# Half of layer 0's output projection by Strassen's products, and three low parts of weight sums split by DMA

## The chip, the cores and the metric

The kernel runs on one core of one Trainium2 chip. The metric is the time of one execution on the device in microseconds (us), the median of several. Engines are named as in the profile: PE is TensorE's matmul, PEld its weight load, DVE is VectorE, ACT is ScalarE, POOL is GpSimd, SP is SyncE, which issues most DMAs.

## The reference

A trunk of two layers over 512 positions (S) with 1024 channels (D), all in float32. In layer 0 a projection gives four quarters of 512 channels; three make a gated convolution y_a, the fourth a multi-scale pooling y_b. Then comes the output projection, and after it the gated FFN with 2816 hidden channels.

```python
def gated_conv_ffn(x, w_gate, w_up, conv_w, conv_b, w_down):
    g = jnp.einsum('bsd,df->bsf', x, w_gate)
    g = causal_dwconv3(g, conv_w) + conv_b
    up = jnp.einsum('bsd,df->bsf', x, w_up)
    return jnp.einsum('bsf,fd->bsd', jax.nn.silu(g) * up, w_down)
...
        xn = rms_norm(h, norm_mix[layer])
...
            mix = jnp.concatenate([y_a, y_b], axis=-1)
            h = h + jnp.einsum('bse,ed->bsd', mix, w_out_even[i])
...
        hn = rms_norm(h, norm_ffn[layer])
        h = h + gated_conv_ffn(hn, w_ffn_gate[layer], w_ffn_up[layer], conv_ffn[layer],
                               b_conv_ffn[layer], w_ffn_down[layer])
```

Layer 1 has another mixer (gated spatial mixing in chunks) with its own output projection, and the same FFN. A last norm ends it.

## The kernel before, in words

**Numbers in two parts.** Every fp32 operand x of a matmul is held as hi, x rounded to the matmul's format, and lo, the rest x - hi. A product is three matmuls: hi·hi, hi·lo, lo·hi (mm3, lines 156 to 159). A split is usually an ACT copy for hi and a DVE subtraction for lo (parts, lines 149 to 154; halves, 791 to 793). The other way, by DMA: ACT writes the negated rounded copy into lo, a DMA issued by POOL adds x onto it (accumulate), ACT writes hi (summed, lines 138 to 146; lines 823 to 825). It takes the subtraction from DVE and gives one copy to ACT and one transfer to the DMA engines.

**The residual stream** h is eight tiles of 128 channels by 512 positions. Weights are fetched on SP's queue, in program order, into four raw buffers of 512 KB ("raw", line 131); a fetch waits until what was read from its buffer before has been used. Parts of weights have six buffers each (whi, wlo).

**Layer 0's mixer** ends with the products pm (y_b, the loop of mm_bank "pm"), the projection group "ab" (b_done: y_a), then project("oe", ...) (project, lines 303 to 317). It runs in two halves of four output tiles; a half is 8 contraction steps by 4 tiles by 3 = 96 matmuls of 512 columns, and its weights are four fetches of 512 KB. When a tile is finished, DVE adds it to h (line 315) and the norm splits the scaled h into hg (hi on ACT, line 202; lo on DVE, 203), squares it on ACT and sums the squares on POOL (213). The FFN's first step follows it on PE without a gap: "gu", FFN tiles 0 and 1 direct, whose fourth contraction step needs the norm's sums. Meanwhile the block sums and the weights of the next group are prepared.

**Seven products.** project_blocks (line 553) does one half of an output projection by Strassen's scheme, with 2 blocks of 256 positions, 2 of 512 input channels and 2 of 256 output channels: seven products instead of eight. Each is for two column blocks 4 steps x 3 = 12 matmuls of 256 columns (multiply, lines 622 to 645, the matmul at 642), 168 in all. It forms four sums of weights on DVE (to), splits seven weights, and adds each finished product onto h in halves of 256 (line 602). The moving operands are halves of the activations and four block sums (block_sums_of, lines 545 to 551, on DVE, in place). Before the change only the second half of layer 1's output projection goes this way ("oo1").

**The FFN** (class Ffn) goes through hidden tiles two at a time, f = 2, 4, ..., 20, each group again by Strassen's products for gate (g) and up (u): prepare(f) fetches four raw tiles (g and u, two halves of the input channels), forms in DVE the weight sums s12 and s34 for g and u, and splits them; products(f) runs the fourteen products in the order g1 u1 g2 g5 g6 u5 u6 g7 u2 u7 g3 u3 g4 u4, and after each an add onto rows or kept (line 865) or a copy (877). s34 holds the weights of products 7 and 3, the last sums to be formed; for up they are formed in the tile of s12 (line 834 and 836). For key "g" and f from 4 on, s12 and s34 are split by DMA; for "u" by ACT and DVE (the choice is by_dma). Where in_both holds (g from 4, u from 6; in group 4 also products 2, 5, 3 of u), a product is 4 matmuls of 512 columns, hi against both parts (line 632), and 4 of 256 with lo (635); else 12 of 256. Between the groups, the down projection takes the finished hidden tiles (d0_..., L157 to L159), with weight parts whi_d and wlo_d (lines 152, 153).

**Order.** Tile's scheduler decides how the instructions of each engine are ordered, from the program text and its own estimates; each engine then runs them strictly in that order, waiting on semaphores. So a change at one place can move instructions elsewhere. Tiles share pools: "four" has 5 buffers of 128 x 2 x 512, "sum" has 3, PSUM has 7 banks.

Of the kernel before, what the change touches and what calls it, by code (L numbers as in the profile page):

```python
# [8 lines left out]
F32 = mybir.dt.float32  # L9
F32R = mybir.dt.float32r  # L10
BF16 = mybir.dt.bfloat16
AF = mybir.ActivationFunctionType
ALU = mybir.AluOpType
PSUM = bass.MemoryType.PSUM

P = 128
D = 1024
S = 512
# [13 lines left out]
def tile_trunk(ctx: ExitStack, tc: tile.TileContext, x, norm_mix, norm_ffn, final_norm,  # L32
# [3 lines left out]
    nc = tc.nc  # L36
    x = x[0]
# [150 lines left out]
    hg = [(t[:, 0], t[:, 1]) for t in hg2]  # L188
# [74 lines left out]
    def split(pool, src, name, scale=1.0, tag="a", bufs=None):  # L263
        hi = pool.tile([P, S], F32R, tag=f"{tag}hi", bufs=bufs, name=f"{name}_hi")
        lo = pool.tile([P, S], F32R, tag=f"{tag}lo", bufs=bufs, name=f"{name}_lo")
        nc.scalar.activation(hi, src, AF.Copy, scale=scale)  # L266
        if isinstance(scale, float):
            nc.vector.tensor_tensor(lo, src, hi.bitcast(F32), ALU.subtract)
        else:
            nc.vector.scalar_tensor_tensor(lo, src, scale, hi.bitcast(F32),  # L270
                                           op0=ALU.mult, op1=ALU.subtract)
        return hi, lo
# [19 lines left out]
    def half_weights(name, w, ks, gi):  # L292

        chunks = {}
        for i in range(0, len(ks), 2):
            k0 = min(ks[i], ks[i + 1])
            hi, lo = weights(
                w[k0 * P : (k0 + 2) * P, gi * 512 : gi * 512 + 512]
                .rearrange("(k p) c -> p k c", p=P), 2, 512, f"{name}_{gi}_{k0}")
            chunks[k0], chunks[k0 + 1] = (hi, lo, 0), (hi, lo, 1)  # L300
        return chunks

    def project(name, w, acts, ks, norm, before=None, halves=(0, 1), tail=4):

        for gi in halves:
            chunks = half_weights(name, w, ks, gi)

            def lhs(k, j):
                hi, lo, n = chunks[k]
                cs = slice(j * P, (j + 1) * P)  # L310
                return hi[:, n, cs], lo[:, n, cs]

            def done(j, ps):
                k = gi * 4 + j
                nc.vector.tensor_tensor(h[k], ps, h[k], ALU.add)  # L315
                if norm is not None:
                    norm.add(k)

            group(f"{name}{gi}", range(4), ks, lhs, lambda k, j: acts[k], tail, done,
                  before if gi == 0 else None)  # L320


    prm0 = prm1 = None
# [10 lines left out]
    def in_group(name, w, c0, lhs_is_weight, on_done, tail, chunks=None, before=None,  # L334
                 after=(None, None), begun=None, after_later=None):
        if chunks is None:
            chunks = {}
            for k in range(0, NK, 2):
                in_parts(chunks, k, in_fetch(name, w, c0, k, 2),
                         after_later if k and after_later else after)  # L340

        def wt(k, j):
            cs = slice(j * P, (j + 1) * P)
            return chunks[k][0][:, cs], chunks[k][1][:, cs]

        def wt_wide(k, j):
            return chunks[k]

        def tokens(k, j):
            cs = slice(j * P, (j + 1) * P)  # L350
            return hg[k][0][:, cs], hg[k][1][:, cs]

        if lhs_is_weight:
            group(name, range(4), list(range(NK)), wt, lambda k, j: hg_k(k), tail, on_done, before,
                  begun=begun)
        else:
            group(name, range(4), list(range(NK)), tokens, wt_wide, tail, on_done, before)

    def mixer0():
        nonlocal prm0  # L360
        w = w_in_even[0]
        with tc.tile_pool(name="m0", bufs=1) as mp:
# [86 lines left out]
            mix = {}  # L449
# [3 lines left out]
            zs = {}  # L453
# [36 lines left out]
            prm0 = params0()  # L490
# [21 lines left out]
            cv = {}  # L512

            def v_done(j, ps):
                p = padded_tile()
                nc.vector.tensor_tensor(p[:, 2:], ps, ac[j], ALU.mult)
                if j % 2 == 0:
                    cv["pair"] = mp.tile([P, 2, S], F32, tag="four", bufs=5, name=f"cv{j}")
                t = cv["pair"][:, j % 2, :]
                conv3(t, p, *(prm0("ca", 4 * i + j) for i in range(3)))  # L520
                nc.gpsimd.tensor_tensor(t, t, rstd[0], ALU.mult)
                cv[j] = t

            in_group("av", w, 1024, True, v_done, 4)

            for g in range(4):
                ps = mm_bank(f"pm{g}")
                mm3(ps, (wpl_hi[:, g, :], wpl_lo[:, g, :]), pooled[g], True, True)
                mix[4 + g] = split(mp, ps, f"yb{g}", scale=prm0("psc", g), tag="mix", bufs=8)

            def b_done(j, ps):
                nc.vector.tensor_tensor(cv[j], ps, cv[j], ALU.mult)
# [2 lines left out]
            in_group("ab", w, 0, True, b_done, 4)  # L535

            nxt = Norm("f0", lambda k: prm0("ffn", k))
            project("oe", w_out_even[0], mix, [4, 5, 6, 7, 0, 1, 2, 3], nxt)
            return nxt


# [3 lines left out]
    def block_sums_of(y0, y1):  # L545

        t3, t1, t2, t4 = y1[:, :, HALF:], y0[:, :, HALF:], y0[:, :, :HALF], y1[:, :, :HALF]
        nc.vector.tensor_tensor(t3, t3, t1, ALU.subtract)
        nc.vector.tensor_tensor(t1, t1, t2, ALU.subtract)
        nc.vector.tensor_tensor(t2, t2, t3, ALU.add)  # L550
        nc.vector.tensor_tensor(t4, t4, t2, ALU.subtract)
# [57 lines left out]
    HALF = S // 2  # L609
    NP = NK // 2  # L610
    PAIRS = [k for i in range(NP) for k in (i, i + NP)]

    FIRST_WIDE = {"g": 4, "u": 6}

    BANK = {1: "a", 6: "a", 7: "a", 4: "a", 5: "e", 3: "e", 2: "b"}

# [36 lines left out]
    class Ffn:  # L653
# [141 lines left out]
        def prepare(self, f):  # L795

            layer, ap, n = self.layer, self.ap, f"{self.layer}_{f}"
            raws = ffn_weights(layer, f, [(key, half) for half in range(2) for key in "gu"])
            stat = {}

            def put(key, product, hi_lo, i):
                stat[key, product] = hi_lo[0][:, i], hi_lo[1][:, i]

            w = self.unit(f"a11_{n}")
            for i, key in enumerate("gu"):
                self.halves(w[0][:, i], w[1][:, i], raws[key, 0][0][:, :, :P])
                put(key, 1, w, i)
            for key in "gu":
                r0, r1 = raws[key, 0][0], raws[key, 1][0]
                s12 = ap.tile([P, 2, 4, P], F32, tag="sum", bufs=3, name=f"s12{key}_{n}")  # L810
                s34 = s12 if key == "u" else ap.tile([P, 2, 4, P], F32, tag="sum", bufs=3,
                                                     name=f"s34{key}_{n}")
                behind(nc.vector.tensor_tensor(s12[:, 0], r0[:, :, P:], r1[:, :, P:], ALU.add),
                       self.added[key])
                nc.vector.tensor_tensor(s12[:, 1], s12[:, 0], r0[:, :, :P], ALU.subtract)
                w = self.unit(f"s12{key}_{n}")

                by_dma = key == "g" and f >= FIRST_WIDE[key]

                def split(w, src):  # L820
                    if not by_dma:
                        return self.halves(*w, src)
                    first = nc.scalar.activation(w[1], src, AF.Copy, scale=-1.0)
                    nc.gpsimd.dma_start(w[1], src, accum_op=ALU.add)
                    behind(nc.scalar.activation(w[0], src, AF.Copy), first)

                def split_s12():
                    split(w, s12)

                hi, lo = summed(*raws[key, 1], between=split_s12,  # L830
                                after=self.first_sums if f == 2 else None)
                put(key, 5, w, 0)
                put(key, 6, w, 1)
                behind(nc.vector.tensor_tensor(s34[:, 0], r0[:, :, :P], r0[:, :, P:],
                                               ALU.subtract), self.added[key])
                nc.vector.tensor_tensor(s34[:, 1], r1[:, :, :P], s12[:, 1], ALU.subtract)
                for i, product in enumerate((2, 4)):
                    c = slice(i * P, (i + 1) * P)
                    stat[key, product] = hi[:, :, c], lo[:, :, c]
                w = self.unit(f"s34{key}_{n}")  # L840
                split(w, s34)
                put(key, 7, w, 0)
                put(key, 3, w, 1)
            return stat

        def products(self, f, stat):
# [12 lines left out]
            def in_both(key, product):  # L859
                return f >= FIRST_WIDE[key] or f == FIRST_WIDE["g"] and product in (2, 5, 3)  # L860

# [642 lines left out]
    n = mixer0()  # L1504
    n = ffn0(n)
    n = mixer1(n)
# [31 lines left out]
```

## Time and profile before

| what | value |
|---|---|
| median of 3 runs | 971.51 us (971.48 to 971.69) |
| the profiled execution | 972.09 us |
| its span, first to last instruction | 970.4 us |
| granted clock of TensorE, mean | 0.998 |
| output projection of layer 0 on PE (oe) | 101.65 to 145.17 us |
| FFN groups 4, 6, 8 of layer 0, with down projections | some 30.6 us each, 188.5 to 280.3 us |

Times in profile rows are us from the start of the span, durations in us or ns. Matmuls overlap in the records: one of 512 columns shows 0.39 us, while the next one starts 0.227 us after it; DVE and ACT instructions in a row overlap by about 0.1 us in the same way. Rows of instructions read: start, duration, engine, line, operation, out<-in, shape, count, and in brackets the idle time before and what ended it. Names are cut of their layer and half, so wlo_s34u is the low part of up's s34 in any group. Rows of groups read: busy us in all, mean ns of one, idle before.

### The profile page before, as it was taken

The numbers are of one execution on the slowest core, as the hardware profiler recorded it, in microseconds if no ns is written. First come the engines' busy times: TensorE is split into PE (matmuls) and PEld (weight loads), VectorE is DVE, ScalarE is ACT, GpSimd is POOL, SyncE is SP. The second block draws the span as 40 slices with busy tenths as digits, with TensorE's granted clock in tenths as the row PEclk, the third lists the DMA queues.
The fourth block names the chain that finished last, engine by engine and source line by source line (L and its number), as shares of the span: only waits on it lengthen the run. The fifth ranks groups of instructions, "written<-read, shape, count | busy, mean of one in ns | idle before, by whom it ended". The sixth has DMA issues, their size and how long they took to land.

```text
span 970.4 us, 13875 instructions
## 1 busy us (share of the span) xinstructions
PE 960.4 (99%) x5024; PEld 821.5 (85%) x5024; DVE 832.9 (86%) x1418; ACT 610.4 (63%) x914; POOL 154.8 (16%) x175
## 2 busy tenths in 40 slices
PE   9999999999999999999999999999999999999996
PEld 7888888988888888888888888989888888888885
DVE  5887458999899898998878689889998989888897
ACT  4623347765575565765487847787665666656675
POOL 2142023110111010110221002311111011100123
PEclk9999999999999999999999999999999999999999
DMA  7442325777777667774352323567767777667775
GB/s 252 138 148 86 87 87 109 167 181 174 195 162 182 156 169 200 155 180 143 130 153 87 109 87 88 141 138 178 184 150 192 191 175 173 164 161 196 196 157 136
DMA packets 93649, 149.39 MB, mean 154 GB/s; under 512 B 5157, under 2 KB 58381, under 8 KB 93581
## 3 DMA queue, kind: packets, MB, share of 16 engines
q1 hardware_dynamic: 77260, 98.69, 32.1%
q0 software_dynamic: 14544, 47.98, 27.5%
q10 hardware_dynamic: 1776, 1.84, 0.6%
q8 instruction: 39, 0.64, 0.3%
q14 instruction: 30, 0.24, 0.1%
HBM read 98.42 MB, written 2.10 MB: 104 GB/s over the span
## 4 chain that ended last, share of the span: by engine, by line
PE 95%; DVE 3%; DMA 1%; issue 1%; ACT 0%; POOLq 0%; DVEq 0%; POOL 0%; ACTq 0%
PE dn L158 3%; PE dn L159 3%; PE dn L157 3%; PE d L158 3%; PE d L157 3%; PE d L159 3%; PE vu_a L1087 2%; PE gu L157 2%; PE gu L159 2%; PE gu L158 2%; PE oe L159 1%; PE oe L158 1%; PE oe L157 1%; PE u_2a L642 1%; PE u_4a L642 1%; PE g_2a L642 1%
## 5 line engine op out<-in xcount | busy, mean ns | idle before, releaser
L144 POOL DMA_DIRECT2D wlo_g<-raw_g x20 | 17.3, 863 | 321.3 <-DVE kept L865 132.5
L678 DVE SCALAR_TENSOR_TENSOR c<-rows,prm,c 128x512 f32<-128x512 f32 x88 | 65.3, 743 | 1.6 <-ACT c L676 1.4
L158 PE MATMUL dn<-wlo_dn,a_hi 128*128 128x512 f32 x144 | 56.2, 390 | 0.0
L158 PE MATMUL d<-a_lo,whi_d 128*128 128x512 f32 x144 | 56.2, 390 | 0.0
L159 PE MATMUL dn<-whi_dn,a_lo 128*128 128x512 f32 x144 | 56.2, 390 | 0.0
L157 PE MATMUL d<-a_hi,whi_d 128*128 128x512 f32 x144 | 56.1, 390 | 0.0
L159 PE MATMUL d<-a_hi,wlo_d 128*128 128x512 f32 x144 | 56.1, 390 | 0.0
L157 PE MATMUL dn<-whi_dn,a_hi 128*128 128x512 f32 x144 | 56.1, 390 | 0.0
L792 ACT ACTIVATE whi_a<-raw_g 128x512 fp32r<-128x512 f32 x20 | 12.6, 632 | 61.5 <-PE g_10e L632 9.3
L142 ACT ACTIVATE wlo_g<-raw_g 128x1024 fp32r<-128x1024 f32 x20 | 21.2, 1062 | 27.5 <-PE g_2e L642 8.8
L676 ACT ACTIVATE c<-rows,prm 128x512 f32<-128x512 f32 x44 | 31.4, 716 | 7.9 <-DVE rows L889 7.7
L686 ACT ACTIVATE s<-c,prm 128x512 f32<-128x512 f32 x44 | 31.4, 716 | 6.2 <-DVE c L678 6.1
L1292 DVE SCALAR_TENSOR_TENSOR y<-dn,small,y 128x512 f32<-128x512 f32 x40 | 28.0, 748 | 8.4 <-PE dn L159 8.4
L202 ACT ACTIVATE hg<-h,prm 128x512 fp32r<-128x512 f32 x24 | 17.3, 720 | 27.1 <-DVE h L315 23.6
L213 POOL TENSOR_TENSOR ssq_f<-ssq_f,sq_f 128x512 f32<-128x512 f32 x14 | 20.9, 1490 | 72.7 <-ACT sq_f L212 37.7
L153 DVE TENSOR_TENSOR wlo_dn<-raw_dn,whi_dn 128x1024 fp32r<-128x1024 f32 x18 | 22.0, 1224 | 11.7 <-ACT whi_dn L152 11.7
L266 ACT ACTIVATE a_hi<-s 128x512 fp32r<-128x512 f32 x40 | 24.9, 627 | 11.3 <-PE d L159 7.7
L159 PEld LDWEIGHTS d<-a_hi,wlo_d 128*128 128x128 f32 x144 | 27.0, 188 | 5.7
L159 PEld LDWEIGHTS dn<-whi_dn,a_lo 128*128 128x128 f32 x144 | 27.0, 188 | 5.7
L157 PEld LDWEIGHTS d<-a_hi,whi_d 128*128 128x128 f32 x144 | 27.1, 188 | 5.4
L158 PEld LDWEIGHTS dn<-wlo_dn,a_hi 128*128 128x128 f32 x144 | 27.0, 188 | 5.4
L157 PEld LDWEIGHTS dn<-whi_dn,a_hi 128*128 128x128 f32 x144 | 27.0, 188 | 5.4
(1131 smaller groups left out, 3309.6 us busy)
## 6 DMA issues: line engine op xcount, KB each, us to landing
raw_g<-in_w_ffn_gate_dram SPq DMA_DIRECT2D x40, 512.0 KB, 4.0
raw_u<-in_w_ffn_up_dram SPq DMA_DIRECT2D x40, 512.0 KB, 4.5
raw_dn<-in_w_ffn_down_dram SPq DMA_DIRECT2D x22, 512.0 KB, 5.9
wlo_g<-raw_g POOLq DMA_DIRECT2D x20, 512.0 KB, 4.5
wlo_u<-raw_u POOLq DMA_DIRECT2D x20, 512.0 KB, 6.3
raw_d<-in_w_ffn_down_dram SPq DMA_DIRECT2D x18, 512.0 KB, 4.1
wlo_s12g<-s12g POOLq DMA_DIRECT2D x18, 512.0 KB, 6.2
wlo_s34g<-s34g POOLq DMA_DIRECT2D x18, 512.0 KB, 6.0
```

The lines of the kernel that those rows point to most:

```text
L142: first = nc.scalar.activation(lo, raw, AF.Copy, scale=-1.0)
L153: behind(nc.vector.tensor_tensor(lo, raw, hi.bitcast(F32), ALU.subtract), after[0])
L157: nc.tensor.matmul(ps, lhs[0], rhs[0], start=start, stop=False)
L158: nc.tensor.matmul(ps, lhs[0], rhs[1], start=False, stop=False)
L159: nc.tensor.matmul(ps, lhs[1], rhs[0], start=False, stop=stop)
L213: nc.gpsimd.tensor_tensor(self.ssq, self.ssq, sq, ALU.add)
L266: nc.scalar.activation(hi, src, AF.Copy, scale=scale)
L642: nc.tensor.matmul(ps, l, r, start=first, stop=end, skip_group_check=True)
L676: nc.scalar.activation(c, t[:, 0:S], AF.Copy, scale=prm("cf", ft))
L678: self.last_conv = nc.vector.scalar_tensor_tensor(c, t[:, i : S + i], prm("cf", i * NF + ft), c, op0=ALU.mult, op1=ALU.add)
L686: self.last_silu = nc.scalar.activation(s, c, AF.Silu, bias=self.prm("bf", ft))
L1292: return nc.vector.scalar_tensor_tensor(dst, ps, ffn.cols[:, t : t + 1], dst, op0=ALU.mult, op1=ALU.add)
```

## The change

The second half of oe goes through project_blocks as "oe1". The first half, project with halves=(0,), calls sums_of at its contraction steps 1 and 2, in which the block sums are formed. The operands are y_a (kept in ya, the pairs cv) and fp32 copies of y_b (ybr, written by ACT beside the split). Two of the four sums go into hg[4..7], which are free until the norm fills them; the other two into eight small tiles t43, split by DMA, 128 KB each. In the FFN of layer 0, the low part of up's s34 is made by DMA in the groups f = 4, 6 and 8.

```diff
@@ mixer0, v_done
                     cv["pair"] = mp.tile([P, 2, S], F32, tag="four", bufs=5, name=f"cv{j}")
+                    ya.append(cv["pair"])
...
+            yb, ya = [], []
             in_group("av", w, 1024, True, v_done, 4)
 
             for g in range(4):
                 ps = mm_bank(f"pm{g}")
                 mm3(ps, (wpl_hi[:, g, :], wpl_lo[:, g, :]), pooled[g], True, True)
                 mix[4 + g] = split(mp, ps, f"yb{g}", scale=prm0("psc", g), tag="mix", bufs=8)
+                if g % 2 == 0:
+                    yb.append(mp.tile([P, 2, S], F32, tag="four", bufs=5, name=f"ybr{g}"))
+                nc.scalar.activation(yb[-1][:, g % 2, :], ps, AF.Copy, scale=prm0("psc", g))
...
-            project("oe", w_out_even[0], mix, [4, 5, 6, 7, 0, 1, 2, 3], nxt)
+            t43 = {}
+
+            def sums_of(k):
+                if k not in (1, 2):
+                    return
+                q = k - 1
+                block_sums_of(ya[q], yb[q])
+                for n in range(2):
+                    kp = 2 * q + n
+                    nc.scalar.activation(hg[4 + kp][0], ya[q][:, n, :], AF.Copy)
+                    nc.vector.tensor_tensor(hg[4 + kp][1], ya[q][:, n, :],
+                                            hg[4 + kp][0].bitcast(F32), ALU.subtract)
+                for i in range(2):
+                    for n in range(2):
+                        at = 4 * q + 2 * i + n
+                        tag, bufs = ("z", 4) if at < 4 else ("zs", 2) if at < 6 else ("pl", 2)
+                        t = mp.tile([P, 2, HALF], F32R, tag=tag, bufs=bufs, name=f"t43_{at}")
+                        src = yb[q][:, n, i * HALF : (i + 1) * HALF]
+                        nc.scalar.activation(t[:, 1], src, AF.Copy, scale=-1.0)
+                        nc.gpsimd.dma_start(t[:, 1], src, accum_op=ALU.add)
+                        nc.scalar.activation(t[:, 0], src, AF.Copy)
+                        t43[i, 2 * q + n] = t[:, 0], t[:, 1]
+
+            project("oe", w_out_even[0], mix, [4, 5, 6, 7, 0, 1, 2, 3], nxt, before=sums_of,
+                    halves=(0,))
+            project_blocks("oe1", w_out_even[0], mix,
+                           {6: lambda kp: tuple(x[:, :HALF] for x in hg[4 + kp]),
+                            5: lambda kp: tuple(x[:, HALF:] for x in hg[4 + kp]),
+                            4: lambda kp: t43[0, kp], 7: lambda kp: t43[1, kp]}, nxt,
+                           mp.tile([P, 4, HALF], F32, tag="four", bufs=5, name="oe_s1"))
...
     FIRST_WIDE = {"g": 4, "u": 6}
+    LATE_START = (4, 6, 8)
...
                 by_dma = key == "g" and f >= FIRST_WIDE[key]
 
-                def split(w, src):
+                def split(w, src, by_dma=by_dma):
                     if not by_dma:
                         return self.halves(*w, src)
...
                 w = self.unit(f"s34{key}_{n}")
-                split(w, s34)
+                split(w, s34, by_dma or layer == 0 and f in LATE_START)
```

By the program's order, on PE nothing moves but oe's second half, single matmuls of u_6b, u_8b and u_10b, and four matmuls of g_6e, which go ahead of u_6a's product 7. On ACT the copy whi_d of a down weight in group 8 goes behind the new copy. On DVE adds, weight subtractions and the sums of the next group change places in groups 6 to 12. SP issues as many DMAs as before.

## The prediction

> **What bounds the kernel now.** I read the page first, then the waits of TensorE, then tables of stages, then single instructions in time. The page:
>
> ```profile
> span 970.4 us, 13875 instructions
> ...
> PE 960.4 (99%) x5024; PEld 821.5 (85%) x5024; DVE 832.9 (86%) x1418; ACT 610.4 (63%) x914; POOL 154.8 (16%) x175
> ...
> q1 hardware_dynamic: 77260, 98.69, 32.1%
> q0 software_dynamic: 14544, 47.98, 27.5%
> ...
> PE 95%; DVE 3%; DMA 1%; issue 1%; ACT 0%; POOLq 0%; DVEq 0%; POOL 0%; ACTq 0%
> ```
>
> PE is busy for 99% of the span and is 95% of the chain that ended last. A microsecond less of matmuls is therefore a microsecond less of time, as long as what feeds PE keeps up; everything else costs only where PE waits. PE's waits between 95 and 340 us, where all of the change lies, are one:
>
> ```profile
> PE g_10a L632 <- DVE rows L865: 0.5, 1, 0.5
> ```
>
> ```profile
> 290.10 0.39 PE L632 MATMUL u_10b<-hg,whi_u 128*128 128x512 f32 x1
> 290.99 1.20 PE L632 MATMUL g_10a<-t,whi_s34g 128*128 128x512 f32 x4 [0.51 <-DVE rows L865]
> ```
>
> The wait is shown as 0.51; by starts it is 290.99 - 290.10 = 0.89 where the next matmul of 512 columns follows after 0.23, so 0.66 us. That is the stall that can go or grow. Stages; columns are the stretch, its length, busy time of PE, PEld (weight load), DVE, ACT and POOL, then clock, DMA share, GB/s:
>
> ```profile
> 101.65:123.41 21.76, 21.76 (x98) 18.02 (x96) 10.23 (x12) 8.11 (x11) 1.71 (x2) 1.00 0.33 97
> 123.41:145.17 21.76, 21.76 (x98) 18.02 (x96) 11.44 (x12) 8.89 (x14) 5.56 (x5) 1.00 0.33 98
> 600.73:620.88 20.15, 20.15 (x169) 20.15 (x168) 19.70 (x27) 11.71 (x16) 6.95 (x5) 1.00 0.65 190
> 188.50:219.20 30.70, 30.70 (x179) 27.03 (x178) 29.09 (x53) 23.11 (x34) 4.31 (x5) 1.00 0.83 186
> 219.20:249.75 30.55, 30.55 (x162) 26.17 (x160) 29.56 (x56) 18.76 (x29) 3.40 (x4) 1.00 0.65 161
> 249.75:280.30 30.55, 30.55 (x162) 26.16 (x161) 27.00 (x51) 18.76 (x29) 2.63 (x4) 1.00 0.73 179
> ```
>
> Rows one and two are the two halves of layer 0's output projection (oe): PE full, DVE half idle. Row three is layer 1's second half, already in the seven-product form. Rows four to six are the FFN groups f = 4, 6, 8, where DVE is full as well (88 to 97%).
>
> **Part 1: the second half of oe by seven products.** Removed: 96 matmuls of 512 columns, 21.76 us. Added: 168 of 256 columns. Their price is in layer 1, the same helper on the same sizes:
>
> ```profile
> 600.89 1.43 PE oo_10a L642 x12
> ...
> 619.60 1.44 PE oo_11a L642 x12
> ```
>
> Fourteen blocks at 1.44 are 20.15 us (the window above), 0.120 us a matmul. So PE saves **21.76 - 20.15 = 1.61 us**, if it is fed. (By columns alone it would be 2.7: the weight loads are busy 20.15 of 20.15 us in that window, so at 256 columns they set the pace.)
>
> What feeds it: DVE gets 8 block sums and 4 low parts of 512 columns, 4 weight sums and 3 more low parts of 1024, and 16 adds of 256 for 4 of 512. With 0.68, 1.22 and 0.42 us (rows of these shapes stand below) that is 8.2 + 8.5 + 4.0 = 20.7 us, some 18.5 net of overlap. The two windows have 11.5 + 10.3 idle, less the 1.6 that go: 20.2. It fits with little left, DVE then being some 96% busy. That is the load of layer 1's window (19.70 of 20.15), where PE did not wait. ACT gets 8 copies of 512 (0.63), 16 of 256 (0.36, a row below), 3 of 1024 (1.06): 14.0 us into 24.9 idle.
>
> ```profile
> L792 ACT ACTIVATE whi_a<-raw_g 128x512 fp32r<-128x512 f32 x20 | 12.6, 632 | 61.5 <-PE g_10e L632 9.3
> ```
>
> POOL issues 8 small accumulating DMAs at 0.86 (rows below), 6.9 us into 34.6 idle; ssq of the norm stands behind them in its queue, and nobody needs it before gu's fourth step, 3 x 12 matmuls of 0.227 or 8 us in. The fetched bytes are the same; 1 MB of small accumulation meets a DMA share of 0.33. I cost all this at nothing: PE's backlog covers it. If DVE falls behind, gu's low parts come late and PE waits: without the 2.2 us of overlap that I counted on (0.08 to 0.1 an instruction), 20.7 would not go into 20.2, which is 0.5 late; layer 1's window shows no wait. Bounds 0 and 0.5, I take 0.
>
> **Part 2: three low parts by DMA.** For f = 4, 6, 8 one subtraction leaves DVE, ACT gets one copy more and POOL one issue more:
>
> ```profile
> L793 DVE TENSOR_TENSOR wlo_s34u<-s12u,whi_s34u 128x1024 fp32r<-128x1024 f32 x4 | 4.9, 1222 | 0.5 <-ACT whi_s34u L792 0.2
> L836 DVE TENSOR_TENSOR s12u<-raw_u,s12u 128x512 f32<-128x512 f32 x4 | 2.7, 684 | 0.0
> ```
>
> DVE is not the last to end there (PE waits for it once, at 290.99), so the 3 x 1.22 us buy nothing at once. What they can buy is that stall; what they can cost is a low part that lands late. ACT's copy comes when s12u is ready, 198.69, 226.13 and 255.86; 1.06 later POOL issues: 199.75, 227.19, 256.9. PE needs the low part at
>
> ```profile
> 206.89 0.28 PE L642 MATMUL u_4a<-t,wlo_s34u 128*128 128x256 f32 x1
> ```
>
> ```profile
> 198.69 1.06 ACT L792 ACTIVATE whi_s34u<-s12u 128x1024 fp32r<-128x1024 f32 x1 [0.80 <-DVE s12u L836]
> ```
>
> ```profile
> 226.13 1.06 ACT L792 ACTIVATE whi_s34u<-s12u 128x1024 fp32r<-128x1024 f32 x1 [0.77 <-DVE s12u L836]
> ```
>
> ```profile
> 232.74 0.63 PE L635 MATMUL u_6a<-t,wlo_s34u 128*128 128x256 f32 x4
> ```
>
> ```profile
> 255.86 1.06 ACT L792 ACTIVATE whi_s34u<-s12u 128x1024 fp32r<-128x1024 f32 x1
> 256.82 1.05 ACT L152 ACTIVATE whi_d<-raw_d 128x1024 fp32r<-128x1024 f32 x1
> 257.77 0.36 ACT L877 COPY rows<-g_8a 128x256 f32<-128x256 f32 x1
> ```
>
> ```profile
> 263.30 0.64 PE L635 MATMUL u_8a<-t,wlo_s34u 128*128 128x256 f32 x4
> ```
>
> that is 7.1, 5.5 and 6.4 us after the issue. In the changed program's own order, four matmuls of g_6e (0.93 us) stand ahead of u_6a's product, so 6.5 in the second. All of a 512 KB accumulation is shown by its neighbours in the same queue:
>
> ```profile
> wlo_s34g<-s34g POOLq DMA_DIRECT2D x4, 512.0 KB, 7.0
> wlo_u<-raw_u POOLq DMA_DIRECT2D x4, 512.0 KB, 7.4
> ```
>
> Those medians would be late by 0 to 1 us. But they hold a queue: in group 8
>
> ```profile
> 248.94 0.86 POOL L824 DMA_DIRECT2D wlo_s34g<-s34g  x1 [1.98 <-ACT wlo_s34g L823]
> 250.83 0.86 POOL L144 DMA_DIRECT2D wlo_u<-raw_u  x1 [1.03 <-ACT wlo_u L142]
> ```
>
> ```profile
> wlo_s34g<-s34g POOLq DMA_DIRECT2D x1, 512.0 KB, 7.6
> ```
>
> ```profile
> wlo_u<-raw_u POOLq DMA_DIRECT2D x1, 512.0 KB, 8.2
> ```
>
> they land at 256.5 and 259.0, 2.5 apart; q0's 27.5% of 970.4 us over 47.98 MB are 2.9 us a piece. So the new one lands 2.5 to 2.9 us behind wlo_u_8 (261.5 to 261.9, 1.4 early) if it has the queue to itself, and up to twice that behind it if it shares with fetches (264.8, 1.5 late). I take no wait, being nearer to the 2.5 of the row; 1.5 stays as a bound. The Trainium skill, "DMA: Bandwidth & Descriptors", section "Anatomy of one DMA — SWDGE (gpsimd) path", fits 2.0 us + bytes/436e3 for such a DMA; by it, an estimate, 3.2 us, nothing would come near to late. The rows of 7.0 and 7.4 do not agree with it here, where the DMAs queue.
>
> **The stall at 290.99** hangs on a chain from a fetch of group 10, on which DVE waits and after which it is full:
>
> ```profile
> 259.61 0.46 SPq L132 DMA_DIRECT2D raw_g<-in_w_ffn_gate_dram  x1
> ```
>
> ```profile
> 264.81 0.69 DVE L813 TENSOR_TENSOR s12g<-raw_g,raw_g 128x512 f32<-128x512 f32 x1 [1.71 <-DMA raw_g<-in_w_ffn_gate_dram]
> 265.42 0.42 DVE L865 TENSOR_TENSOR kept<-u_8b,kept 128x256 f32<-128x256 f32 x1
> ...
> 289.38 1.22 DVE L153 TENSOR_TENSOR wlo_d<-raw_d,whi_d 128x1024 fp32r<-128x1024 f32 x1
> 290.52 0.42 DVE L865 TENSOR_TENSOR rows<-g_10a,rows 128x256 f32<-128x256 f32 x1
> ```
>
> In the changed order two of these instructions leave the stretch before g_10a's add: wlo_d moves behind it (1.14 by starts) and one add of u_8b ahead of the fetch (0.33): **-1.47**. Against it: whi_d (256.82) now stands behind ACT's additional copy, its wlo_d frees the buffer for that fetch, so it is issued **+0.9** later; and the fetch shares the DMA engines with the new accumulation, **0 to +2.9**, of which groups 4 and 6 give back about 1.1, as DVE, full until the four adds of down's sums, reaches group 8's sums one subtraction earlier. Sum: 0.66 - 1.47 + 0.9 + (-1.1 to 1.8), so 0 to 1.9; the middle, 0.45, differs from 0.66 by less than I can know. I take the stall as it is, change 0.
>
> **Sum**: profiled 972.09 (span 970.4 and 1.7 around it) - 1.61 = 970.48; on the median of 971.51, 0.58 below that run, **969.9 us**.
>
> **Rivals.**
> 1. *The stall goes too*: the fetch isn't slowed, 0.66 more: 969.24, say 969.1 to 969.6. For it: the two instructions gone, 1.47 > 0.9. Against: the shared DMA engines.
> 2. *A wait at u_8a or a longer one at g_10a*: DMA share there is high already:
>
> ```profile
> 251.00:265.00 14.00, 14.00 (x82) 12.19 (x81) 10.45 (x19) 6.87 (x12) 0.69 (x1) 1.00 0.95 257
> ```
>
> 0.95 of 14 us leaves 0.7 for another 2.9. A wait at u_8a of up to 1.5 lets DVE catch up and so is not added to the one at g_10a; the larger of 1.5 and 1.9 less 0.66 is at most +1.24, so 970.0 to 971.2; with a second group late by half a microsecond or so, up to 972. The Trainium skill, the same page, "Queues, rings and completion order", says that each engine goes round between its queues packet by packet; by that rule the fetch and the accumulation would each go at half pace while both last. No row of this profile shows the two alone, so it stays a rival.
> 3. *Slower*: accumulations late in all three groups. With landing L after the issue, PE waits (L - 7.1) + (L - 6.5) + (L - 6.4); with 1.61 gained this costs time from L = 7.2 and over 0.2% (1.94 us, about the least that measurements of this kernel tell from no change) from 7.9. With 9.5 for each,
>
> ```profile
> wlo_s34g<-s34g POOLq DMA_DIRECT2D x1, 512.0 KB, 9.5
> ```
>
> (the worst, in group 6), 3 x 9.5 - 20.0 = 8.5 us: 978.4. For it the medians of 7.0 and 7.4; against it that of those in group 8 the one was issued 1.9 us behind the other, and the new one is issued 6.1 behind it (256.9 - 250.83).
> 4. *Columns are the price*: 168 x 0.1134 = 19.05, gain 2.71: 968.8. The Trainium skill, "TensorE: Matmul & The Clock Gate", section "Back-to-back issue gap", has 262 cycles for 256 columns; an estimate of 168 x 0.109 = 18.3 us comes from it. Layer 1's row of 1.44 for 12 speaks against both.
>
> **Numbers.** Forecast 0.45; rival 1 0.22; rival 2 0.20; rival 3 0.10; rival 4 0.03. The range from 969.1 to 972.0 leaves out rivals 3 and 4 and ends of others. Faster by over 0.2% is below 969.57, slower above 973.45: faster 0.30 (rivals 1 and 4 and some of the forecast), slower 0.12, the rest 0.58.
>
> **What would show it.** oe1: fourteen blocks of 1.44 and gu's first matmul 20.15 us after oe1's, without a wait; a wait there means DVE. wlo_s34u landing 5 to 6.5 us after each issue; a wait of u_4a, u_6a or u_8a for a DMA is rival 2 or 3. The wait at g_10a between 0 and 1.9, for DVE's rows, with the fetch of raw_g_10 landing at 264 to 266 (less 1.6). The prediction is wrong if PE waits for anything else, or if later groups, whose order also moves, lose time.

## The result and the profile after

| | median us (runs) | against before, 95% interval |
|---|---|---|
| before | 971.51 (13) | |
| after | 973.96 (13) | 1.0022, 1.0013 to 1.0030 |

By the medians the changed kernel is 2.45 us slower; by the ratio it is 2.1 (1.3 to 2.9). 969.9 was forecast, 969.1 to 972.0 as the range. The page of after:

```profile
span 971.7 us, 14106 instructions
...
PE 959.7 (99%) x5096; PEld 823.3 (85%) x5096; DVE 847.9 (87%) x1446; ACT 624.9 (64%) x944; POOL 163.7 (17%) x186
...
q1 hardware_dynamic: 78284, 98.69, 32.0%
q0 software_dynamic: 16128, 50.60, 29.0%
...
PE 85%; DVE 9%; DMA 2%; ACT 2%; issue 1%; POOL 0%; DVEq 0%; POOLq 0%; ACTq 0%
```

PE's busy time is 0.7 us less, and yet the span is longer. PE's share of the chain that ended last fell from 95% (99% in a second profile of before, see below) to 85%: where PE waits, the chain runs through DVE, ACT and DMAs. All waits of PE that the list shows:

```profile
PE clock L61 <- DVE idle L56: 1.3, 1, 1.3
PE g_10a L667 <- DVE rows L900: 0.7, 1, 0.7
PE u_6a L670 <- DMA wlo_s34u<-s12u: 0.6, 1, 0.6
PE u_8a L670 <- DMA wlo_s34u<-s12u: 0.3, 1, 0.3
```

The prediction had leaned on a single profile of the kernel before. In a second one (span 969.4, time 971.09, the median of the kernel before on that chip) PE has no wait at g_10a at all:

```profile
PE clock L61 <- DVE idle L56: 1.3, 1, 1.3
PE z L441 <- ACT hg L409: 0.3, 1, 0.3
```

So the stall of 0.66 us that the prediction kept as it is was not always there. DVE's chain is just in time for g_10a, and a few tenths of a microsecond in a landing decide: in group 8, wlo_u took 8.2 us in the first profile and 7.8 in the second. The comparison below is with this second profile. The table has the starts of the same matmuls in after less those in before, so it says where time came and went; the end is counted from the start of the last matmul:

| stretch | change, us |
|---|---|
| up to oe | +0.08 |
| oe, both halves (43.52 to 41.91) | -1.61 |
| group 6 (the wait at u_6a) | +1.02 |
| group 8 (the wait at u_8a) | +0.78 |
| group 10 (the wait at g_10a) | +1.18 |
| from there to the last matmul | +0.06 |
| from the last matmul to the end (8.50 to 9.29) | +0.79 |
| sum | +2.30 |

By starts a wait is some 0.16 us longer than the list has it, since matmuls overlap in the records. Small waits for DVE's adds, which the list leaves out, make up most of the rest in groups 8 and 10 (0.23 and 0.25 us at u_8a and u_10a).

**Part 1 on PE** is as forecast, to 0.01 us. oe1's blocks of matmuls (start, duration):

```profile
123.39 1.43 PE oe_10a L677 x12
124.83 1.44 PE oe_11a L677 x12
```

and the window of oe1 (columns as in the prediction): DVE is busy for 18.46 of 20.18 us, and PE has no wait.

```profile
123.20:143.38 20.18, 20.18 (x169) 20.15 (x168) 18.46 (x27) 11.32 (x16) 5.67 (x4) 1.00 0.53 158
```

**Part 2.** The new DMAs take 5.7, 6.7 and 6.5 us from issue to landing in groups 4, 6 and 8:

```profile
wlo_s34u<-s12u POOLq DMA_DIRECT2D x1, 512.0 KB, 5.7
```

```profile
226.06 0.86 POOL L859 DMA_DIRECT2D wlo_s34u<-s12u  x1 [7.32 <-ACT wlo_s34u L858]
...
256.45 0.86 POOL L859 DMA_DIRECT2D wlo_s34u<-s12u  x1 [5.32 <-ACT wlo_s34u L858]
```

```profile
wlo_s34u<-s12u POOLq DMA_DIRECT2D x1, 512.0 KB, 6.7
```

```profile
wlo_s34u<-s12u POOLq DMA_DIRECT2D x1, 512.0 KB, 6.5
```

PE wanted the second at 232.01 and the third at 262.52 (0.93 us after the start of the first of the four hi matmuls), and started with them at 232.79 and 262.94:

```profile
231.08 1.09 PE L667 MATMUL u_6a<-t,whi_s34u 128*128 128x512 f32 x4
232.79 0.74 PE L670 MATMUL u_6a<-t,wlo_s34u 128*128 128x256 f32 x4 [0.62 <-DMA wlo_s34u<-s12u]
```

```profile
261.59 1.09 PE L667 MATMUL u_8a<-t,whi_s34u 128*128 128x512 f32 x4
262.94 0.74 PE L670 MATMUL u_8a<-t,wlo_s34u 128*128 128x256 f32 x4 [0.26 <-DMA wlo_s34u<-s12u]
```

The copy on ACT that comes before each of them ends 0.30 us before POOL issues the DMA:

```profile
224.70 1.06 ACT L858 ACTIVATE wlo_s34u<-s12u 128x1024 fp32r<-128x1024 f32 x1 [1.11 <-DVE s12u L871]
255.09 1.06 ACT L858 ACTIVATE wlo_s34u<-s12u 128x1024 fp32r<-128x1024 f32 x1
```

The DMA engines are full meanwhile. In the 6.8 us of group 6's transfer (226.0 to 232.8), q1 (fetches) and q0 (POOL's) have, in packets, MB and share of 16 engines:

```profile
q1 hardware_dynamic: 1537, 1.53, 67.6%
q0 software_dynamic: 144, 0.52, 39.2%
q8 instruction: 1, 0.02, 0.8%
```

This transfer had its own queue to itself (wlo_u had landed at 224.80) and still needed 6.7 us. Four fetches were in flight beside it, issued at 224.10, 224.94, 229.49 and 230.62. The two queues did not share the engines evenly; they took turns. The three views that follow are 227.4 to 228.4, 229.0 to 230.8 and 231.5 to 232.8 (a share of over 100% can be read as full):

```profile
q1 hardware_dynamic: 373, 0.38, 109.7%
```

```profile
q0 software_dynamic: 92, 0.38, 105.9%
```

```profile
q1 hardware_dynamic: 450, 0.45, 104.1%
q0 software_dynamic: 3, 0.01, 3.3%
```

So the accumulation moved behind the two fetches ahead of it. Three packets of it are left in the last view. All others had ended at 231.45, these follow one another until 232.38, so one engine seems to lag by 0.9 us. The one packet of q8 (228.82 to 229.75, 0.9 us) fell into this transfer; what it is comes below.

The fetch of group 10 on which DVE waits lands later, too. The wait on it is 3.01 us, where the two profiles of before have 1.71 and 1.02:

```profile
265.88 0.69 DVE L848 TENSOR_TENSOR s12g<-raw_g,raw_g 128x512 f32<-128x512 f32 x1 [3.01 <-DMA raw_g<-in_w_ffn_gate_dram]
```

### The profile page after: what moved, and what is told of

The parts are those of the page before. It is cut to its first block, busy times and chain, and to the rows that moved or that the text cites. A ratio compares the mean times of both kernels' runs of the same rounds, so it can differ in the third digit from the quotient of the medians.

```text
span 971.7 us, 14106 instructions
## 1 busy us (share of the span) xinstructions
PE 959.7 (99%) x5096; PEld 823.3 (85%) x5096; DVE 847.9 (87%) x1446; ACT 624.9 (64%) x944; POOL 163.7 (17%) x186
## 4 chain that ended last, share of the span: by engine, by line
PE 85%; DVE 9%; DMA 2%; ACT 2%; issue 1%; POOL 0%; DVEq 0%; POOLq 0%; ACTq 0%
PE dn L158 3%; PE dn L159 3%; PE dn L157 3%; PE d L158 3%; PE d L159 3%; PE d L157 3%; PE vu_a L1122 2%; DMA raw_g<-in_w_ffn_gate_dram 1%; PE vu_e L1122 1%; PE dn_a L1421 1%; DVE c L713 1%; PE gu L157 1%; PE u_20a L667 1%; PE u_16a L667 1%; PE u_12a L667 1%
## 5 line engine op out<-in xcount | busy, mean ns | idle before, releaser
L202 ACT ACTIVATE hg<-h,prm 128x512 fp32r<-128x512 f32 x24 | 17.2, 718 | 23.4 <-DVE h L315 16.9
L158 PEld LDWEIGHTS d<-a_lo,whi_d 128*128 128x128 f32 x144 | 27.0, 188 | 5.4
```

Of the source, the lines that this page charges most:

```text
L158: nc.tensor.matmul(ps, lhs[0], rhs[1], start=False, stop=False)
```

## The experiments

Ratios are to the kernel before on the same chip; behind them stands the 95% interval.

**Before once more**, the profile used above:

> The kernel before once more, for a second profile: the wait at g_10a and the first 101 us vary from run to run. Expected: span 969.3 to 970.4, POOL's DRAIN 6.74 again, the wait at g_10a between 0 and 0.7.

Measured: span 969.4, DRAIN 6.73, no wait at g_10a.

**Which part costs?** Part 1 alone: `LATE_START = ()` in after.

> The seven products alone, without the three low parts by DMA (LATE_START empty). Theory A, all of the loss comes from the three accumulating DMAs: PE keeps the 1.6 us of part 1 and has no wait but the one at g_10a, of about the size of before (0.5 to 0.9); time 969.6 to 970.3 us. Theory B, the seven products cost something of their own beyond the profile shown so far (order or DMA of the groups after it): 971 us or more.

Measured: 971.09, ratio 1.0000 (0.9992 to 1.0009). Part 1 alone neither gains nor loses measurably, which is not what theory A had. By the profile, oe gives its 1.61 us, and they are given back at two places where nothing was changed: a wait at g_10a,

```profile
PE g_10a L667 <- DVE rows L900: 0.8, 1, 0.8
```

(0.96 us more than in the second profile of before, in group 10), and 0.54 us behind the last matmul (8.50 to 9.04).

Part 2 alone, before with the `split(w, s34, by_dma or layer == 0 and f in LATE_START)` of the change:

> The three low parts by DMA alone, oe as before. Theory A: PE waits for wlo_s34u in groups 6 and 8 and longer at g_10a, 1.1 to 2.7 us more than before in the profile; time 972.6 to 975.6 us. Theory B: within 0.5 us of before, 971.0 to 972.0.

Measured: 975.27, ratio 1.0044 (1.0030 to 1.0058), and the waits that theory A names, with one more, at g_6a:

```profile
PE u_6a L636 <- DMA wlo_s34u<-s12u: 1.0, 1, 1.0
PE g_10a L633 <- DVE rows L866: 0.7, 1, 0.7
PE u_8a L636 <- DMA wlo_s34u<-s12u: 0.6, 1, 0.6
PE g_6a L633 <- DVE rows L866: 0.4, 1, 0.4
```

The two parts do not simply add up: part 2 costs 0.44% alone and 0.22% on top of part 1. Most of the difference is in group 6 (1.92 us against 0.98 by starts), where the wait at g_6a comes on top and the DMA is issued 0.5 us later.

**Which group?** `LATE_START = (4,)` and `LATE_START = (10,)` in after:

> The seven products and the low part by DMA in group 4 alone (LATE_START = (4,)). Theory A: this one landed 0.3 us before its use, and its transfer is over before group 10's fetches; time that of the seven products alone within 0.5 us. If group 4 alone already costs 1 us or more, lateness at the use is not the cause and the load on the DMA engines or the moved order is.

Measured: 970.74, ratio 1.0000 (0.9991 to 1.0009), one wait of 0.5 at g_10a. Group 4 alone costs nothing that can be measured: there the DMA lands in time (5.8 us after its issue).

> The seven products and the low part by DMA in group 10 alone, where the DVE subtraction stands in front of the add that PE waits for. Theory A: DVE reaches g_10a's add 1.1 us sooner, the wait there goes, 0.5 to 0.9 us less than the seven products alone (968.9 to 969.7), unless the low part lands late at u_10a (issue about 287, needed about 293), then 970 to 971.5.

Measured: 972.71, ratio 1.0016 (1.0007 to 1.0025). The wait at g_10a is gone from the list, as DVE has no subtraction ahead of the add, but the low part takes 7.0 us and PE waits for it at u_10a:

```profile
PE u_10a L670 <- DMA wlo_s34u<-s12u: 1.6, 1, 1.6
```

One wait was traded for a larger one.

**The DMA or the moved order?** After without the accumulating transfer:

```diff
-                    nc.gpsimd.dma_start(w[1], src, accum_op=ALU.add)
+                    if not (key == "u" and layer == 0):
+                        nc.gpsimd.dma_start(w[1], src, accum_op=ALU.add)
```

> The whole change, but the accumulating DMA of wlo_s34u in groups 4, 6, 8 is left out (the negated copy stays in its place, so this part of the result is not the reference's). All orders of ACT and DVE stay. Theory A, landing late and load on the DMA engines make the loss of part 2: no wait at u_6a and u_8a, at g_10a at most 0.5, time 0 to 0.9 us below the seven products alone, 970.2 to 971.1. Rival, the moved order or ACT's three copies make it: waits of 1 us or more remain, 972.5 or more.

This kernel leaves the low part's addition out; its times alone are of use. Measured: 970.39, ratio 0.9993 (0.9984 to 1.0002); PE has no wait but the first. Three transfers of 512 KB make the difference between this kernel and after: 3.0 us between the two profiled spans (968.6 and 971.7), 2.8 by the ratios, and 0.24 of it in the end of the program, see below. The moved order does not cost: DVE starts on group 10 about as late here as in part 1 alone (15.1 and 15.4 us after g_8a's first matmul), and yet the wait at g_10a is gone. So DVE's relief does what the prediction hoped for, up to 0.8 us in group 10 (+0.18 against +0.96 by starts); in the time it is 0.7 us at most, within the intervals. With the three transfers group 10 is at +1.18 all the same.

**The end of the program.** Behind the last matmul the norm's arithmetic and the output DMAs are as before. But POOL's sequencer ends with an instruction named DRAIN, and the last semaphore steps of all engines come behind it. In the trace it takes longer the more DMAs POOL has issued: 6.73 us for 101 (both profiles of before), 6.98 for 104, 7.38 for 109, 7.47 for 110, 7.63 for 112 (after). In before it ends 0.6 us after SP's last wait, in after 1.5. Two kernels test this. The small operands t43 split without POOL:

```diff
-                        nc.scalar.activation(t[:, 1], src, AF.Copy, scale=-1.0)
-                        nc.gpsimd.dma_start(t[:, 1], src, accum_op=ALU.add)
                         nc.scalar.activation(t[:, 0], src, AF.Copy)
+                        nc.vector.tensor_tensor(t[:, 1], src, t[:, 0].bitcast(F32), ALU.subtract)
```

> The seven products alone, their eight small operands t43 split by ACT and DVE instead of by eight accumulating DMAs of POOL (LATE_START empty). Theory C: the wait of POOL at the very end of the program (its DRAIN, 6.74 us with 101 POOL DMAs, 7.38 with 109, 7.63 with 112) lengthens by 0.08 us for each DMA that POOL issued; it is back at 6.74 here and the time 0.6 us below that of the seven products alone, 970.3 to 970.7, unless the 3 us more on DVE make PE wait. Theory D, the end of the program is no matter of these DMAs: DRAIN stays near 7.4 and the time at 971.1.

Measured: 971.59, ratio 1.0003 (0.9995 to 1.0012). DRAIN is 6.73, back as theory C says, and the end 8.39 us behind the last matmul, 0.65 less than in part 1 alone. But the 3 us more on DVE cost 1.0 us by starts ahead of group 6 (0.18 in oe, 0.33 in group 2, 0.52 in group 4), of which the list shows g_4a. The wait at g_10a is that of part 1 alone, and the one at z stands in before too:

```profile
PE g_10a L666 <- DVE rows L899: 0.9, 1, 0.9
PE z L441 <- ACT hg L409: 0.3, 1, 0.3
PE g_4a L666 <- DVE rows L899: 0.3, 1, 0.3
```

And before with 24 idle DMAs of POOL:

```diff
+            for n in range(24):
+                behind(nc.gpsimd.dma_start(spare24[:, n : n + 1], ones), masked)
```

> The kernel before with 24 more DMAs of POOL of 512 bytes each, issued in layer 1's mixer where POOL has nothing else to do for 60 us; everything else keeps its order. They copy a constant into a tile that nobody reads. Theory C: DRAIN at the end 6.74 + 24 x 0.081 = 8.7 us, time 1.9 us above before (973.0 to 973.4). Theory D: DRAIN 6.7, time as before within 0.3 us.

Measured: 970.69, ratio 0.9994 (0.9985 to 1.0003). Theory C's straight line fell: DRAIN is 3.92 with 125 DMAs, not 8.7. The end comes 7.90 us behind the last matmul instead of 8.50; SP, which waits for the output DMAs, is then the last. So a shorter DRAIN shows at the end of the trace too, though the time's 0.4 us are within the interval. Two more counts, one run each:

> The kernel before with 8 small DMAs of POOL in layer 1's mixer: 109 POOL DMAs in all, as many as with the seven products, but none of them early. If DRAIN at the end goes by their number up to some point, 0.08 us each, it is 7.4 us as in the seven products alone; if it goes by the pause in which they fall, it is under 6.7.

> 16 small DMAs, 117 in all. By number: 8.0 us if it still grows, or already falling to the 3.9 that 125 gave. By the pause: under 6.7.

Measured: 109 DMAs, DRAIN 7.26 (span 969.3); 117, DRAIN 3.43 (span 968.3). At 109 it is nearly that of part 1 alone (7.38), whose eight DMAs stand elsewhere and are larger, so the number counts more than place and size. DRAIN grows by 0.06 to 0.08 us for each DMA from 101 to 112 and from 117 to 125, and falls by 4 us between 112 and 117 and by 1.6 between 125 and 133 (2.28, below). Kernels with 137 and 161 did not fit into the on-chip memory, so higher counts are not known. What makes the steps stays open.

**The wait at g_10a.** In part 1 alone all DMAs of POOL and SP from 20 us ahead of g_8a's first matmul to 9 us behind it are issued at the same distance from it as in before, to 0.01 us. Yet wlo_s34g and wlo_u of group 8 land later. Transfers that begin in that stretch, before (second profile), then part 1 alone:

```profile
q0 software_dynamic: 432, 1.57, 59.4%
q1 hardware_dynamic: 1093, 1.59, 31.5%
...
wlo_s34g<-s34g POOLq DMA_DIRECT2D x1, 512.0 KB, 7.2
wlo_u<-raw_u POOLq DMA_DIRECT2D x1, 512.0 KB, 7.8
```

```profile
q0 software_dynamic: 432, 1.57, 59.0%
q1 hardware_dynamic: 1103, 1.57, 31.7%
q8 instruction: 1, 0.02, 0.4%
...
wlo_s34g<-s34g POOLq DMA_DIRECT2D x1, 512.0 KB, 8.2
wlo_u<-raw_u POOLq DMA_DIRECT2D x1, 512.0 KB, 8.9
```

The one new line is q8, a packet of 16 KB. The trace has 39 such packets in before and 40 in after and in part 1 alone. PE has 10,048 instructions in before and 10,192 in after, weight loads counted, which is about 256 to a packet: the packets would be blocks of PE's program. Each takes about 1 us on a DMA engine. A transfer that is spread over all 16 engines lands with the last of them, so one block in its way could cost it up to 1 us. In before the blocks come 7.5 us ahead of g_8a and 15.4 behind it, outside these transfers; oe1 adds 144 instructions of PE, and the second one comes 5.1 us behind. raw_u of group 10 waits for wlo_u (it is issued 10.1 us after g_8a instead of 9.0), raw_g stands behind it in SP's queue, DVE waits for raw_g, and PE for DVE. That is a theory (theory E); a longer warm-up of PE, which moves the blocks and nothing else, tests it.

> The kernel before with 60 more matmuls in PE's warm-up (68 of 64 columns for 8 of 512), nothing else moved: PE's instruction stream is 120 instructions longer ahead of everything. Theory E: PE's instructions come in blocks of 16 KB (256 instructions) by a DMA that holds one of the 16 DMA engines for 1 us; where that block falls between 3 and 6 us after g_8a starts, it lies in front of wlo_s34g and wlo_u of group 8, which land 0.7 to 1 us later, and so do the next fetches, DVE's chain and g_10a. In before the block came 7.5 us ahead of g_8a and 15.8 behind; 120 instructions move the latter to about 5 behind. Expected: wlo_s34g of group 8 takes 8.0 to 8.3 us (7.2 to 7.6 before), raw_u of group 10 is issued 10 us after g_8a (9.0 to 9.4), the wait at g_10a is 0.8 to 1.0 by the records. Rival F, the later landing of the kernels with oe1 comes from something else: 7.1 to 7.6 us, wait 0 to 0.5 as in before. The whole time is also longer by what the warm-up takes more.

Measured: 972.18, ratio 1.0012 (1.0003 to 1.0021). The block came 8.2 us behind g_8a, not 5, so after wlo_s34g and in wlo_u:

```profile
q8 instruction: 1, 0.02, 0.4%
...
wlo_s34g<-s34g POOLq DMA_DIRECT2D x1, 512.0 KB, 7.3
wlo_u<-raw_u POOLq DMA_DIRECT2D x1, 512.0 KB, 9.2
```

```profile
PE g_10a L632 <- DVE rows L865: 1.1, 1, 1.1
```

wlo_s34g is as in before, wlo_u 1.4 us longer than in the second profile (1.0 than in the first), and the kernel before, with nothing else moved, has a wait at g_10a like that of part 1 alone.

> The seven products alone, with 70 more matmuls in PE's warm-up (78 of 64 columns), 140 instructions. The block that came 5 us behind the start of g_8a moves to 7 or 8 us ahead of it. Theory E: wlo_s34g of group 8 lands after 7.1 to 7.6 us and the wait at g_10a (0.8 in the seven products alone) is 0 to 0.5. Rival F: it lands after 8.2 and the wait stays.

Measured: 973.45, ratio 1.0021 (1.0012 to 1.0030). No block comes within 8 us of g_8a ahead or 12 behind:

```profile
wlo_s34g<-s34g POOLq DMA_DIRECT2D x1, 512.0 KB, 7.2
wlo_u<-raw_u POOLq DMA_DIRECT2D x1, 512.0 KB, 8.2
```

and the wait at g_10a is gone from PE's list (0.1 is left), so theory E holds in both directions, in one profile each. The time is nevertheless longer. The span is 971.0 against 969.5 in part 1 alone, 0.6 us by the later oe and the rest by other waits:

```profile
PE g_2a L677 <- ACT rows L912: 0.7, 1, 0.7
PE g_4a L667 <- DVE rows L900: 0.3, 1, 0.3
```

so this is a test and no remedy. Besides, 1.8 to 3.3 us of this kernel's time lie outside the span. In the kernel before it is 1.7 to 1.8, in most runs of part 1 alone and of its versions with idle DMAs 1.9 to 2.1; why is not known.

The other profiles bear theory E out, with a smaller price. In eleven of them (before twice, with 8, 16 and 24 idle DMAs and with the longer warm-up; part 1 alone, with group 4, without POOL's DMAs, with the longer warm-up and with idle DMAs) the wait at g_10a is the time from g_8a's first matmul to DVE's start on raw_g, less 14.55 us, to 0.02 us. DVE starts after 14.2 to 15.1 us in the six without a block in the two transfers, 14.5 in the mean, and after 14.8 to 15.6 in the five with one, 15.2 in the mean. So a block costs some 0.7 us there, and landings vary by as much without one: the first profile of before had its stall with no block near.

**A version that beats both.** Part 1 alone with the 24 idle DMAs:

> The seven products alone with the 24 small DMAs of POOL in layer 1's mixer, after which POOL's DRAIN at the end was 3.9 instead of 6.7 us in the kernel before. If DRAIN counts the DMAs since then, it is 3.9 here too, the end of the program is set by the output's DMAs, 7.9 us after the last matmul instead of 9.1, and the time is 1.2 us below the seven products alone: 969.7 to 970.1. If the small DMAs help only by chance, 971.

Measured: 969.58, ratio 0.9986 (0.9977 to 0.9995). DRAIN is 2.28, the end 8.07 us behind the last matmul instead of 9.04. In this profile the wait at g_10a is 0.2. And with another order of fetches in `prepare`:

```diff
-            raws = ffn_weights(layer, f, [(key, half) for half in range(2) for key in "gu"])
+            raws = ffn_weights(layer, f, [(key, half) for key in "gu" for half in range(2)])
```

> As the run with the seven products and 24 small DMAs, and SP fetches the halves of gate ahead of those of up (g0 g1 u0 u1 for g0 u0 g1 u1) in every FFN group; no other engine's order moves. In group 10 gate's second half is then issued when wlo_u of group 8 has landed, 0.5 us sooner, and ahead of up's first half; DVE, which waits for it 2 us, starts 0.5 to 1.5 us sooner and the wait at g_10a (0.8) goes: 0.5 to 0.9 below that run, 968.9 to 969.4. If up's halves are then late somewhere, PE waits at u products and nothing is gained.

Measured: 969.11, ratio 0.9979 (0.9970 to 0.9988), 1.9 us faster than before. The 0.5 us against the run with the old order are not clear of noise, as the two intervals overlap. DVE finds raw_g there (idle 0.07 us, not shown in its row), although a block falls into these transfers here too (3.0 us behind g_8a):

```profile
260.90 0.69 DVE L849 TENSOR_TENSOR s12g<-raw_g,raw_g 128x512 f32<-128x512 f32 x1
```

PE has no wait left in the FFN.

## Why the prediction was wrong

The measured median lies 4.1 us above the forecast. By the table above, the loss is in group 6 (1.02), group 8 (0.78), group 10 (1.18) and the end of the program (0.79); the prediction had put all four at nothing.

- *Part 1 saves 1.61 us on PE and is fed*: right to 0.01 us, and the busy DVE (18.46 of 20.18) did not make PE wait. DVE got 16.1 us more in the two windows of oe, where 18.5 were reckoned.
- *"I cost all this at nothing"*: wrong, though not by what was weighed there. Eight more DMAs of POOL cost 0.5 to 0.6 us in DRAIN at the end (0.8 with the eleven of after). And 144 more instructions of PE moved a block of its program into the way of group 8's accumulations, which cost 0.96 us at g_10a in that profile and some 0.7 in the mean. Neither has a row in the prediction that carries its price; the sum took what lies behind the last matmul as given.
- *"I take no wait"*, since *"the new one lands 2.5 to 2.9 us behind wlo_u_8"*: the step that failed. The three DMAs landed 4.8, 8.0 and 3.8 us behind wlo_u, and PE waited 0.78 and 0.43 us by starts for the second and third. The 2.5 us between two landings was that of transfers already in flight together; in group 6 the new one was issued 1.3 us behind the landing of wlo_u and found two fetches ahead of it. The bound named in the prediction, 1.5 late in group 8, held.
- *"1.06 later POOL issues"*: too early. POOL issues 0.29 us after ACT's copy has ended, in before in 84 of 85 accumulations of this kind. In group 6 DVE's sum was 0.33 us later as well. So PE needed the low parts 6.0 and 6.1 us after the issue, and not 6.5 and 6.4; with the issues where the prediction had them, the same landings would have been late by some 0.1 us each, an estimate from these rows. In group 6 a block of PE's program came on top: without the 0.9 us by which one engine lagged, that transfer would have been 0.2 us early. But no block is needed: in part 2 alone none fell there, the DMA was issued 0.5 us later still and took 7.1 us, and PE waited 1.2 us by starts.
- *"I take the stall as it is, change 0"*: wrong. The working gave 0 to 1.9 and the wait grew to 0.7 by the records. raw_g of group 10 was issued 1.2 us later after g_8a than in the second profile of before (10.75 against 9.59) and took longer. DVE began with it 2.5 us later (16.9 against 14.4), of which 0.9 did not reach PE. And the wait at u_8a did not let DVE catch up as rival 2 had it, since the chain starts at a fetch that the same transfers delay: the losses of groups 6, 8 and 10 added up (1.02, 0.78, 1.18). Without the three transfers, with all orders as in after, group 10 is at +0.18.
- *The base*: the sum was made against a profile with a stall that the second profile does not have. Against the second one, the 0.66 of "the stall goes too" was never there to gain.
- *Rivals*: rival 2 was nearest to the mechanism, with a price of up to 2.1 us above the forecast where groups 6, 8 and 10 lost 3.0, because it took the larger of two waits and not their sum. Of rival 3, lateness in all three groups, group 4 did not come true. Half pace for both queues, as rival 2 worked it out from the rule of the Trainium skill that an engine goes round between its queues ("DMA: Bandwidth & Descriptors", "Queues, rings and completion order"), is not what group 6 shows: for 1.0 us all 373 packets were q1's, and then for 1.8 us all 92 were q0's. The fit of 3.2 us for such a DMA by itself (the same page of the Trainium skill, "Anatomy of one DMA — SWDGE (gpsimd) path") does not agree with the 5.7 to 6.7 us measured beside fetches, nor with 4.5 us, the median of wlo_g in before.

## What to carry to other kernels

Where DMA engines are full, taking an operation from a busy engine to a DMA moves the wait. The budget for it runs from the end of what the DMA waits for to the landing of the transfer among those that run beside it; the gap between two landings is not that budget. A gain on PE of 0.2% is as large as what a shifted instruction stream or a few more POOL DMAs can cost elsewhere: look at what ends last behind the last matmul, and at a second profile of the kernel before, ahead of the sum. A chain that is just in time can be loosened at its root as well as by relieving the engine at its end: here the order of two fetches took the wait at g_10a away and added no transfer.

## What the runs showed of the hardware

- PE's program comes in packets of 16 KB for 256 instructions, each some 1 us on a DMA engine. A 512 KB accumulation in whose way one falls lands later: wlo_u of group 8 took 7.8 to 8.2 us in the six profiles of before and part 1 without a block there, and 8.2 to 9.2 in the five with one.
- Where fetches and an accumulation were in flight together, they took turns: in group 6 of after all 373 packets of 1.0 us were the fetches', then all 92 of 1.8 us the accumulation's.
- POOL issues an accumulating DMA 0.29 us after the end of the ACT copy that it waits for (84 of 85 in before).
- POOL's DRAIN at the end of the program takes 6.73 us with 101 POOL DMAs and 7.63 with 112, but 3.43 with 117, 3.92 with 125 and 2.28 with 133; 24 more DMAs that do nothing brought the end of the kernel before from 8.50 to 7.90 us behind the last matmul.
- At 256 columns a matmul takes 0.120 us in layer 0 as in layer 1, more than half of the 0.227 of 512 columns; the weight loads are then busy for 20.15 of 20.18 us.
